# A two-layer hybrid decoder trunk on one core: the state-space products' small blocks as 256-column operands, and PSUM as four single and two double banks

## The chip, the cores and the metric

The kernel runs on one core of a Trainium2 chip. The metric is the time of one execution on the device, in microseconds (us); a smaller one is better.

## What is computed

A sequence of 512 tokens of width 2048 goes through two layers. Layer A is sparse attention: an indexer of 16 small heads scores all earlier tokens, each query keeps its best 128, and 16 heads attend over those. Layer B is a Mamba-2 mixer with 64 heads of width 64 and chunks of 128 tokens. The change touches the diagonal part of B's scan and a few accumulators of A. What B computes there is, from the reference:

```python
a_cs = jnp.cumsum(a_, axis=-1)
lmat = jnp.exp(segsum(a_))
cb = jnp.einsum('bclgn,bcsgn->bgcls', c_, b_)
y_diag = jnp.einsum('bgcls,bgrcls,bcsgrp->bclgrp', cb, lmat, x_)
...
return (y_diag + y_off).reshape(b, s, nh, p)
```

The kernel works with chunks of 256 tokens there (two blocks of 128), so a head has for each of two chunks an upper block (source tokens 0 to 127 of the chunk, 256 target tokens) and a small block (source tokens 128 to 255, 128 target tokens). The indexer of layer A, which the change touches as well, is

```python
dots = jnp.einsum('bqhd,bsd->bqsh', iqb, ik)
score = jnp.einsum('bqsh,bqh->bqs', jax.nn.relu(dots), iwb).astype(jnp.float32)
```

## The kernel before, in words

**Products.** Every float32 product is made of reduced-precision parts: an operand is split into a high part (a ScalarE copy) and a low part (a VectorE subtraction), and TensorE forms high·high, low·high and high·low. Most of the work are dense tiles of 128 output rows by 512 tokens, class `Dense`: 16 or 32 blocks of the inner dimension, three products each (L229 to L231), accumulated in one PSUM tile `acc`. Four such tiles at a time are made token by token for the values v (class `TokenMajor`, L265 to L267).

**Order.** The program is written out by hand: a main loop over units of four blocks, in which one tick is one block (`kk`). At each tick generator threads are stepped, which emit the evictions, the attention and the state-space work between the dense products. `yield n` puts off a thread by n ticks. Each engine runs its instructions in the order written, and the framework adds the semaphore waits. Weights are loaded by SyncE's queue into three `raw` buffers and split three units ahead (L206 on ScalarE, L90 on VectorE).

**PSUM.** Eight banks of 512 float32 columns in one pool, each tile one bank (`PS`, L77): `acc`, the indexer's `dots`, the attention's `sps`, `ptp`, `av`, the state-space tiles `xst`, `st`, `yo`, `cpa`, `cpb`, and `y0`, `y1`, `yc`. A new tile waits until the last reader of the bank's former tile is done.

**The places that matter here.**

- The first five dense tiles (indexer queries) are made together, unit by unit. As each ends, `evac_iq` (L382 to L390) copies and subtracts its upper and its lower 64 rows in turn: `iqa`, two ticks later `iqb`.
- `index_thread` (L406 on): for each of three query blocks and 16 heads one `dots` tile of two products (L424, L425), one tick later its relu on ScalarE (L428), two ticks later its share of the score on VectorE (L434).
- `TokenMajor.mm` (L259): the four token blocks b have an accumulator each. After the last unit's products of block b its eviction is emitted at once: `vh` on ScalarE (L498), two ticks later `vl` on VectorE (L500).
- `m_make` (L843) builds the mask tiles of head pair p, m = 0 and 1 for the upper blocks of both chunks, m = 2 for the two small blocks, splits each into `mh` and `ml`. `m_mul` (L874), when m = 2 is there, forms all products of the pair: eight into `y0` and `y1` (L886, L887), six into `yc` (L892 to L894), each of 256 columns. A pair's 128 rows of a stationary operand hold one head's high part in 64 and its low part in the other 64, so one product gives both. VectorE adds the pieces up (L906 and two adds a head).

Of the kernel before, what the change touches and what calls it, by code (L numbers as in the profile page):

```python
# [16 lines left out]
P = 128  # L17
# [25 lines left out]
def kernel(  # L43
# [23 lines left out]
    banks = ctx.enter_context(tc.tile_pool(name="banks", bufs=8, space=bass.MemoryType.PSUM))  # L67
# [9 lines left out]
    def PS(name):  # L77
        return banks.tile([P, S], F32, tag="s", name=name)

# [94 lines left out]
    class Dense:  # L174
        def __init__(self, src, ncol, nk, operand, evac, t0=0, t1=S, packed=False, early=None,
                     order=None, keep=(), given=None):
# [37 lines left out]
        def mm(self, u, kk):  # L214
            first = u == self.order[0] and kk == 0
            if first:
                self.acc = PS("acc")
            ts, m = slice(self.t0, self.t1), self.ncol
            out = self.acc[:, : self.t1 - self.t0]
            held = self.given.w if self.given and u in self.given.keep else self.w  # L220
            w = [a[:, kk] for a in held[u]]
            k = 4 * u + kk
            xh, xl = self.operand(k)
            last = u == self.order[-1] and kk == 3
            if self.packed:
                te.matmul(out[: 2 * m], w[2], xh[:, ts], start=first, stop=last, skip_group_check=True)
                te.matmul(out[:m], w[0], xl[:, ts], start=False, stop=last, skip_group_check=True)
            else:
                te.matmul(out[:m], w[0], xh[:, ts], start=first, stop=False)  # L229
                te.matmul(out[:m], w[0], xl[:, ts], start=False, stop=False)  # L230
                te.matmul(out[:m], w[1], xh[:, ts], start=False, stop=last)  # L231
            if kk == 3 and u not in self.keep:
                del held[u]
            if last:
                run(self.evac(out if self.packed else out[:m]))

    class TokenMajor:
# [168 lines left out]
    def index_thread(iw):  # L406
# [9 lines left out]
        for i in range(1, NB):  # L416
# [369 lines left out]
    def xdt_make(p, d2):  # L786
# [14 lines left out]
        highs, lows = (slice(0, 4, 3), slice(0, 2)), (slice(1, 3), slice(2, 4))  # L801
        for c in range(2):
            sc.copy(out=parts[c][:, :, highs[c]], in_=heads2(v)[:, c:4:2])
        yield HOP
        for c in range(2):
            sub(parts[c][:, :, lows[c]], heads2(v)[:, c:4:2], f(parts[c][:, :, highs[c]]))
# [36 lines left out]
    def m_make(p, m):  # L843
# [19 lines left out]
        hi, lo = T("mh", F32R), T("ml", F32R)  # L863
        yield 1
        yield from split(hi, lo, t)
# [8 lines left out]
    def m_mul(p, m, hi, lo):  # L874
        m_next[0] = (p, m + 1) if m < 2 else (p + 1, 0)
        m_tiles.setdefault(p, []).append((hi, lo))
        if m == 2:
            tiles_m = m_tiles.pop(p)
            ys, yc = [PS("y0"), PS("y1")], PS("yc")
            stat = lambda s, n: xdt[p][s % 2][:, 256 * (s // 2) + P * n : 256 * (s // 2) + P * (n + 1)]  # L880
            two = lambda a: a.rearrange("p (e l) -> p e l", e=2)
            for s, (hi, lo) in zip((0, 2), tiles_m):
                for e in range(2):
                    x = stat(s, e)
                    out = ys[e][:, 128 * s : 128 * s + 256]
                    te.matmul(out, x, hi[:, 256 * e : 256 * e + 256], start=s == 0, stop=False, skip_group_check=True)  # L886
                    te.matmul(out, x, lo[:, 256 * e : 256 * e + 256], start=False, stop=True, skip_group_check=True)  # L887
# [15 lines left out]
            odd = lambda a: a.rearrange("p (c h l) -> p c h l", h=2, l=P)  # L903
            for e in range(2):
                r, q = slice(64 * e, 64 * e + 64), slice(64 - 64 * e, 128 - 64 * e)
                ve.scalar_tensor_tensor(out=v[r], in0=x[r], scalar=col(C_D, p)[r], in1=ys[e][r],  # L906
                                        op0=ALU.mult, op1=ALU.add)
                yield 1
                add(v[r], v[r], ys[e][q])
                yield 1  # L910
                add(odd(v[r])[:, :, 1], odd(v[r])[:, :, 1], odd(yc[r])[:, :, e])
# [59 lines left out]
    def evac_ob(j):  # L971
        def go(ps):
            t = PS("x2p") if j >= KD - 5 else T("x2")
# [57 lines left out]
    EARLY_TILES = 5  # L1031
    for t in range(8):
        dense(wa[t], P, 16, opA, evac_iq(t), t0=P, early=t if t < EARLY_TILES else None)
# [219 lines left out]
```

## Time and profile before

| | |
|---|---|
| median of 3 executions | 2420.07 us (2419.6 to 2422.0) |
| the profiled execution | 2420.4 us, its span 2418.7 us |
| TensorE (PE) busy | 2403.6 us, 99% of the span |
| VectorE (DVE) busy | 1564.1 us, 65% |
| ScalarE (ACT) busy | 1060.4 us, 44% |
| granted TensorE clock, mean | 0.999 of full speed |

The profile comes from one execution. Matrix products overlap each other in it (a product of 512 columns is shown as 0.39 us long, but the next starts 0.23 us after it), so what a product costs is read from start to start. PEld is the loading of the stationary operand. "Idle before" is the time an engine stood still just before an instruction, with the instruction that ended it.

### The profile page before, as it was taken

To read this page: it belongs to the slowest core of one execution; us is meant where nothing else is said; L and a number is where in the kernel's file an instruction comes from. 1 tells how busy PE (TensorE), PEld (TensorE's weight loads), DVE (VectorE), ACT (ScalarE), POOL (GpSimd) and SP (SyncE) were. 2 spreads that over 40 slices of the span, in tenths; PEclk is the share of its full clock that TensorE was granted. 3 is DMA by queue.
4 is the path that set the end of the run, shared out by engine and by line. 5 is a ranking of instruction groups with operands and counts; after the bars stand their busy time and mean duration, and the time that the engine had idled before them with its cause. 6 is when DMAs were issued, how large, how long until landed. Compare 5 with 4: busy or idle time off the path is not lost.

```text
span 2418.7 us, 29767 instructions
## 1 busy us (share of the span) xinstructions
PE 2403.6 (99%) x11430; PEld 2019.1 (83%) x11430; DVE 1564.1 (65%) x2811; ACT 1060.4 (44%) x2102; POOL 1.2 (0%) x8
## 2 busy tenths in 40 slices
PE   9999999999999999999999999999999999999998
PEld 9888888888888888888888888888888888888887
DVE  6569455464554664448788888888888888433334
ACT  6433233232332443334556565565656566322222
POOL 0000000000000000000000000000000000000000
PEclk9999999999999999999999999999999999999999
DMA  6362222222222223433333333333334344332233
GB/s 223 101 131 88 107 93 80 85 91 89 93 81 84 90 105 135 152 118 126 128 104 125 118 122 123 127 128 102 125 111 140 114 148 157 127 113 100 101 113 109
DMA packets 83439, 278.53 MB, mean 115 GB/s; under 512 B 7745, under 2 KB 40929, under 8 KB 58209
## 3 DMA queue, kind: packets, MB, share of 16 engines
q1 hardware_dynamic: 78976, 266.41, 32.6%
q10 hardware_dynamic: 4320, 10.23, 1.2%
q8 instruction: 89, 1.46, 0.2%
q14 instruction: 54, 0.43, 0.1%
HBM read 258.32 MB, written 18.02 MB: 114 GB/s over the span
## 4 chain that ended last, share of the span: by engine, by line
PE 96%; DMA 2%; DVE 1%; ACT 0%; ACTq 0%; SPq 0%; issue 0%; DVEq 0%
PE acc L229 27%; PE acc L231 27%; PE acc L230 27%; PE acc L265 2%; PE acc L267 2%; PE acc L266 2%; DMA raw<-wa 2%; PE ptp L547 1%; PE y L887 1%; PE y L886 1%; PE xst L789 1%; DMA rawu<-wa 0%; PE av L563 0%; PE sps L518 0%; PE av L562 0%; PE sps L517 0%
## 5 line engine op out<-in xcount | busy, mean ns | idle before, releaser
L90 DVE TENSOR_TENSOR wl<-raw,wh 128x512 fp32r<-128x512 f32 (+1 forms) x788 | 528.5, 684 | 136.8 <-ACT wh L206 95.2
L206 ACT CAST wh<-raw 128x512 fp32r<-128x512 f32 (+1 forms) x724 | 426.3, 613 | 176.1 <-PE acc L230 100.9
L229 PE MATMUL acc<-x1h,wh 128*128 128x512 f32 x1280 | 503.1, 393 | 0.0
L230 PE MATMUL acc<-x1l,wh 128*128 128x512 f32 x1280 | 499.2, 390 | 0.0
L231 PE MATMUL acc<-x1h,wl 128*128 128x512 f32 x1280 | 498.9, 390 | 0.0
L229 PE MATMUL acc<-xh,wh 128*128 128x512 f32 (+2 forms) x912 | 353.0, 387 | 1.8 <-ACT wh L206 1.5
L231 PE MATMUL acc<-xh,wl 128*128 128x512 f32 (+2 forms) x912 | 349.4, 383 | 0.4 <-DVE wl L90 0.3
L230 PE MATMUL acc<-xl,wh 128*128 128x512 f32 (+2 forms) x912 | 349.2, 383 | 0.5 <-DVE xl L101 0.5
L231 PEld LDWEIGHTS acc<-x1h,wl 128*128 128x128 f32 x1280 | 240.3, 188 | 51.0
L229 PEld LDWEIGHTS acc<-x1h,wh 128*128 128x128 f32 x1280 | 240.7, 188 | 46.5
L230 PEld LDWEIGHTS acc<-x1l,wh 128*128 128x128 f32 x1280 | 240.8, 188 | 46.2
L229 PE MATMUL acc<-ygh,wh 128*128 128x512 f32 (+1 forms) x544 | 205.3, 377 | 0.0
L231 PE MATMUL acc<-ygh,wl 128*128 128x512 f32 (+1 forms) x544 | 204.9, 377 | 0.0
L230 PE MATMUL acc<-ygl,wh 128*128 128x512 f32 (+1 forms) x544 | 204.9, 377 | 0.0
L231 PEld LDWEIGHTS acc<-xh,wl 128*128 128x128 f32 (+1 forms) x912 | 170.6, 187 | 34.7 <-DVE wl L90 2.3
L229 PEld LDWEIGHTS acc<-xh,wh 128*128 128x128 f32 (+1 forms) x912 | 170.7, 187 | 32.0 <-ACT wh L206 2.1
L230 PEld LDWEIGHTS acc<-xl,wh 128*128 128x128 f32 (+1 forms) x912 | 170.9, 187 | 30.1 <-DVE xl L101 1.4
L231 PEld LDWEIGHTS acc<-ygh,wl 128*128 128x128 f32 x544 | 102.4, 188 | 18.8
L229 PEld LDWEIGHTS acc<-ygh,wh 128*128 128x128 f32 x544 | 102.4, 188 | 18.8
L230 PEld LDWEIGHTS acc<-ygl,wh 128*128 128x128 f32 x544 | 102.4, 188 | 18.5
L697 DVE SCALAR_TENSOR_TENSOR hh<-rw,cols,hh 128x511 f32<-128x511 f32 x144 | 107.4, 746 | 6.5 <-ACT hh L694 4.0
L857 ACT ACTIVATE bc<-bc,aloc 128x256 f32<-128x256 f32 (+1 forms) x256 | 102.8, 446 | 0.5
(279 smaller groups left out, 3297.3 us busy)
## 6 DMA issues: line engine op xcount, KB each, us to landing
raw<-wb SPq DMA_DIRECT2D x80, 1024.0 KB, 4.8
raw<-wa SPq DMA_DIRECT2D x48, 1024.0 KB, 4.9
raw<-wbo SPq DMA_DIRECT2D x33, 1024.0 KB, 4.8
bc<-r_scr SPq DMA_DIRECT2D x96, 256.0 KB, 6.1
raw<-wav SPq DMA_DIRECT2D x16, 1024.0 KB, 4.9
raw<-wao SPq DMA_DIRECT2D x16, 1024.0 KB, 5.2
yg_scr<-yy SPq DMA_DIRECT2D x24, 256.0 KB, 4.4
ygr<-yg_scr SPq DMA_DIRECT2D x24, 256.0 KB, 5.1
```

Source lines behind the costliest of these rows:

```text
L90: ve.tensor_tensor(out=out, in0=a, in1=b, op=ALU.subtract)
L206: sc.copy(out=self.w[u][0], in_=self.raw[u].rearrange("p (k j) -> p k j", k=4))
L229: te.matmul(out[:m], w[0], xh[:, ts], start=first, stop=False)
L230: te.matmul(out[:m], w[0], xl[:, ts], start=False, stop=False)
L231: te.matmul(out[:m], w[1], xh[:, ts], start=False, stop=last)
L265: te.matmul(out, xh[:, bs], wh, start=u == 0, stop=False)
L266: te.matmul(out, xh[:, bs], wl, start=False, stop=False)
L267: te.matmul(out, xl[:, bs], wh, start=False, stop=u == 15)
L547: te.transpose(ps[:, n + (i - j) * P : n + (i - j + 1) * P], prob[i][:, j * P : (j + 1) * P], ident)
L697: ve.scalar_tensor_tensor(out=hh[:, d:], in0=rw[:, : S - d], scalar=col(C_CW, 4 * ct + 3 - d), in1=hh[:, d:], op0=ALU.mult, op1=ALU.add)
L789: te.transpose(ps[:, c * P : (c + 1) * P], xs[p][:, c * P : (c + 1) * P], ident)
L857: sc.activation(out=t3[:, e, a:b], in_=t3[:, e, a:b], func=AF.Relu, scale=-1.0, bias=aloc[:, s, 2 * p + e : 2 * p + e + 1])
```

## The change

- `m_make` for m = 2 writes two tiles `m0` and `m1`, one a head, in which high and low part of each chunk's small block lie side by side: 256 columns for a chunk. That takes two ScalarE copies and two VectorE subtractions of 256 columns in place of one each of 512.
- `m_mul` forms four products with them in place of six. Each adds its high half to the second 128 columns of the upper block, and leaves its low half in 128 columns of its own. A head's results for a chunk take 384 columns of a bank, so `y` is two tiles of two banks.
- `xdt_make` writes the stationary parts in the same order for both chunks.
- PSUM becomes four single banks and two double ones (`PS2`). Besides `y`, the double ones hold: the first four dense tiles, two to a tile (`half_of_two`); the four accumulators of `TokenMajor`; the `dots` of two heads, whose four products are now emitted together; and four late tiles of the output projection's residual.

```diff
+    banks = ctx.enter_context(tc.tile_pool(name="banks", bufs=4, space=bass.MemoryType.PSUM))
...
+    def PS2(name):
+        return banks.tile([P, 2, S], F32, tag="y", name=name, bufs=2)
...
-                self.acc = PS("acc")
+                self.acc = self.bank() if self.bank else PS("acc")
...
-                self.acc = [PS("acc") for _ in range(NB)]
+                self.acc = [a[:, b] for a in (PS2("vacc"), PS2("vacc")) for b in range(2)]
...
-                q = iqhl[h // 2][h % 2]
-                qs = slice((i - 1) * P, i * P)
-                ps = PS("dots")
-                te.matmul(ps[:, :w], q[:, qs], hi[:, :w], start=True, stop=False)
-                te.matmul(ps[:, :w], q[:, qs], los[h % 2][:, :w], start=False, stop=True)
+                if h % 2 == 0:
+                    qs = slice((i - 1) * P, i * P)
+                    two = PS2("dots")
+                    for e in range(2):
+                        q = iqhl[h // 2][e]
+                        te.matmul(two[:, e, :w], q[:, qs], hi[:, :w], start=True, stop=False)
+                        te.matmul(two[:, e, :w], q[:, qs], los[e][:, :w], start=False, stop=True)
+                ps = two[:, h % 2]
...
+            hi, lo = T("m0", F32R), T("m1", F32R)
+            cut = lambda a: a.rearrange("p (c x l) -> p c x l", c=2, x=2)
+            src = t.rearrange("p (e c l) -> p e c l", e=2, c=2)
+            for e, a in enumerate((hi, lo)):
+                sc.copy(out=cut(a)[:, :, 0], in_=src[:, e])
+            yield HOP
+            for e, a in enumerate((hi, lo)):
+                sub(cut(a)[:, :, 1], src[:, e], f(cut(a)[:, :, 0]))
...
-            hi, lo = tiles_m[2]
-            for i, s in enumerate((1, 3)):
-                ls, out = slice(i * P, (i + 1) * P), two(yc[:, 256 * i : 256 * i + 256])
-                te.matmul(out, stat(s, 0), two(hi)[:, :, ls], start=i == 0, stop=False, skip_group_check=True)
-                te.matmul(out, stat(s, 0), two(lo)[:, :, ls], start=False, stop=False, skip_group_check=True)
-                te.matmul(out, stat(s, 1), two(hi)[:, :, ls], start=False, stop=i == 1, skip_group_check=True)
+            for c in range(2):
+                for e in range(2):
+                    te.matmul(ys[e][:, c, P : 3 * P], stat(2 * c + 1, e), tiles_m[2][e][:, 256 * c : 256 * c + 256],
+                              start=False, stop=True, skip_group_check=True)
...
+    both = []
+    def half_of_two():
+        if not both:
+            a = PS2("acc2")
+            both.extend([a[:, 0], a[:, 1]])
+        return both.pop(0)
```

**Place 1: TensorE, the last unit of the first four v accumulators.** Names are output<-operands, with buffer numbers; brackets name the semaphores that an instruction waits for, by the engine that counts them. Before, each block has a tile of its own:

```order
L265 MATMUL acc_2313<-wh_2538,xh_423 128x512 [waits Activation_49]
L266 MATMUL acc_2313<-wl_2539,xh_423 128x512 [waits DVE_49]
L267 MATMUL acc_2313<-wh_2538,xl_424 128x512
L265 MATMUL acc_2314<-wh_2538,xh_423 128x512
L266 MATMUL acc_2314<-wl_2539,xh_423 128x512
```

And now:

```order
L270 MATMUL vacc_2287<-wh_2510,xh_421 128x512 [waits Activation_49]
L271 MATMUL vacc_2287<-wl_2511,xh_421 128x512 [waits DVE_49]
L272 MATMUL vacc_2287<-wh_2510,xl_422 128x512
L270 MATMUL vacc_2287<-wh_2510,xh_421 128x512 [waits Activation_49]
L271 MATMUL vacc_2287<-wl_2511,xh_421 128x512
L272 MATMUL vacc_2287<-wh_2510,xl_422 128x512
L270 MATMUL vacc_2288<-wh_2510,xh_421 128x512
L271 MATMUL vacc_2288<-wl_2511,xh_421 128x512
L272 MATMUL vacc_2288<-wh_2510,xl_422 128x512
L270 MATMUL vacc_2288<-wh_2510,xh_421 128x512 [waits Activation_49]
```

The products stand in the same order. The first product of the second half of each double tile has a wait for ScalarE that it did not have.

**Place 2: TensorE, the last unit of the second indexer tile.** Before:

```order
L229 MATMUL acc_203<-xh_372,wh_489 128x384 [waits Activation_49]
L230 MATMUL acc_203<-xl_373,wh_489 128x384
L231 MATMUL acc_203<-xh_372,wl_490 128x384 [waits DVE_49]
L229 MATMUL acc_203<-xh_388,wh_489 128x384
L230 MATMUL acc_203<-xl_389,wh_489 128x384
```

And now, where tiles one and two are halves of `acc2_175`:

```order
L234 MATMUL acc2_175<-xh_370,wh_487 128x384 [waits Activation_49]
L235 MATMUL acc2_175<-xl_371,wh_487 128x384
L236 MATMUL acc2_175<-xh_370,wl_488 128x384 [waits DVE_49]
L234 MATMUL acc2_175<-xh_386,wh_487 128x384 [waits Activation_49]
L235 MATMUL acc2_175<-xl_387,wh_487 128x384
L236 MATMUL acc2_175<-xh_386,wl_488 128x384
L234 MATMUL acc2_175<-xh_405,wh_487 128x384
L235 MATMUL acc2_175<-xl_406,wh_487 128x384
L236 MATMUL acc2_175<-xh_405,wl_488 128x384
L234 MATMUL acc2_175<-xh_421,wh_487 128x384 [waits DVE_49]
```

The second and the fourth block of this unit have a wait now. The fourth tile, second half of `acc2_229`, has the same three.

**Place 3: TensorE, the indexer's `dots` of the second query block, heads 4 and 5.** Before, the even head's two products stand between dense ones, the odd head's two follow nine dense products later, and none of the four has a wait:

```order
L230 MATMUL acc_1409<-xl_373,wh_1405 128x512
L231 MATMUL acc_1409<-xh_372,wl_1406 128x512 [waits DVE_49]
L424 MATMUL dots_1509<-ikh_992,iqa_587 128x384
L425 MATMUL dots_1509<-ikla_993,iqa_587 128x384
L229 MATMUL acc_1409<-xh_388,wh_1405 128x512
L230 MATMUL acc_1409<-xl_389,wh_1405 128x512
```

And now:

```order
L235 MATMUL acc_1399<-xl_371,wh_1395 128x512
L236 MATMUL acc_1399<-xh_370,wl_1396 128x512 [waits DVE_49]
L431 MATMUL dots_1497<-ikh_990,iqa_585 128x384 [waits Activation_49]
L432 MATMUL dots_1497<-ikla_991,iqa_585 128x384
L431 MATMUL dots_1497<-ikh_990,iqb_586 128x384
L432 MATMUL dots_1497<-iklb_992,iqb_586 128x384
L234 MATMUL acc_1399<-xh_386,wh_1395 128x512
L235 MATMUL acc_1399<-xl_387,wh_1395 128x512
```

The odd head's two products moved up by nine dense products to the even head's, and the first of the four waits for ScalarE: the tile lies where `dots_1406`, heads 0 and 1, lay two tiles before.

## Rows read from the trace of the kernel before

**Rows 1.** The page: engines' busy time (share, instructions), and the chain's shares.

```profile
PE 2403.6 (99%) x11430; PEld 2019.1 (83%) x11430; DVE 1564.1 (65%) x2811; ACT 1060.4 (44%) x2102; POOL 1.2 (0%) x8
PE 96%; DMA 2%; DVE 1%; ACT 0%; ACTq 0%; SPq 0%; issue 0%; DVEq 0%
```

**Rows 2.** Busy time of a stretch: stretch, its length, PE, PEld, DVE, ACT.

```profile
1200.00:1900.00 700.00, 698.85 (x3405) 589.16 (x3403) 594.35 (x1003) 422.97 (x861) 0.00 (x0) 1.00 0.35 121
```

**Rows 3.** PE's waits: line, releaser, us in total, times, longest.

```profile
PE st L822 <- DVE xd2l L90: 1.1, 1, 1.1
```

**Rows 4.** Timeline of PE, one head pair's products: start, length, instruction.

```profile
1161.35 0.28 PE L886 MATMUL y<-mh,xdhl 128*128 128x256 f32 x1
...
1163.02 0.40 PE L229 MATMUL acc<-x1h,wh 128*128 128x512 f32 x1
```

**Rows 5.** Groups of instructions by line: xcount, busy us, mean ns, idle before.

```profile
L93 ACT CAST mh<-bc 128x512 fp32r<-128x512 f32 x96 | 59.6, 621 | 36.7 <-DVE bc L862 36.3
L803 ACT CAST xdhl<-xdt 128x256 fp32r<-128x256 f32 x64 | 22.7, 401 | 44.1 <-DVE xdt L793 44.1
L90 DVE TENSOR_TENSOR ml<-bc,mh 128x512 fp32r<-128x512 f32 x96 | 65.7, 685 | 6.9 <-ACT mh L93 5.5
L90 DVE TENSOR_TENSOR xdhl<-xdt,xdhl 128x256 fp32r<-128x256 f32 x64 | 24.1, 418 | 0.0
L892 PE MATMUL yc<-mh,xdhl 128*128 128x256 f32 x64 | 18.1, 283 | 0.0
```

**Rows 6.** Timeline of PE and ACT at the end of the first v tiles.

```profile
282.31 0.39 PE L267 MATMUL acc<-wh,xl 128*128 128x512 f32 x1
282.54 0.39 PE L265 MATMUL acc<-wh,xh 128*128 128x512 f32 x1
282.74 2.73 ACT L498 ACTIVATE vh<-acc,rcol 128x512 fp32r<-128x512 f32 x4 [24.92 <-PE acc L267]
```

**Rows 7.** Timeline of PE at the wait for late weights.

```profile
152.63 0.49 PE L229 MATMUL acc<-xh,wh 128*128 128x512 f32 x1 [1.03 <-ACT wh L206]
152.96 0.40 PE L230 MATMUL acc<-xl,wh 128*128 128x512 f32 x1
```

**Rows 8.** Timeline at the end of the first five tiles: starts of tiles two, three, five.

```profile
43.10 0.33 PE L229 MATMUL acc<-xh,wh 128*128 128x384 f32 x1
45.18 0.33 PE L229 MATMUL acc<-xh,wh 128*128 128x384 f32 x1
49.34 0.34 PE L229 MATMUL acc<-xh,wh 128*128 128x384 f32 x1
```

**Rows 9.** Timeline of ACT there: copies of tiles one, one, two, three, three.

```profile
43.30 0.47 ACT L386 CAST iqa<-acc 64x384 fp32r<-64x384 f32 x1 [6.42 <-PE acc L231]
...
44.39 0.47 ACT L386 CAST iqb<-acc 64x384 fp32r<-64x384 f32 x1
45.44 0.47 ACT L386 CAST iqa<-acc 64x384 fp32r<-64x384 f32 x1 [0.57 <-PE acc L231]
...
48.14 0.47 ACT L386 CAST iqa<-acc 64x384 fp32r<-64x384 f32 x1
...
49.46 0.47 ACT L386 CAST iqb<-acc 64x384 fp32r<-64x384 f32 x1 [0.32 <-DVE iqa L90]
```

**Rows 10.** Timeline of SyncE's queue, then ACT, then PE, around the late weights.

```profile
114.83 0.66 SPq L367 DMA_DIRECT2D bias_scr<-rs  x1
115.58 81.80 SPq L187 DMA_DIRECT2D raw<-wa  x7
...
151.96 0.62 ACT L206 CAST wh<-raw 128x512 fp32r<-128x512 f32 x1 [11.59 <-DMA raw<-wa]
152.48 0.48 ACT L428 ACTIVATE relu<-dots 128x384 f32<-128x384 f32 x1
...
148.68 0.33 PE L424 MATMUL dots<-ikh,iqa 128*128 128x384 f32 x1
```

**Rows 11.** Busy time of the stretch behind it, columns as in rows 2.

```profile
152.80:172.00 19.20, 19.10 (x83) 14.87 (x84) 18.72 (x52) 7.84 (x18) 0.00 (x0) 1.00 0.29 107
```

More of the change, by code (lines that the diff above doesn't have):

```diff
@@ L66 @@
     small = ctx.enter_context(tc.tile_pool(name="small", bufs=24))
-    banks = ctx.enter_context(tc.tile_pool(name="banks", bufs=8, space=bass.MemoryType.PSUM))
+    banks = ctx.enter_context(tc.tile_pool(name="banks", bufs=4, space=bass.MemoryType.PSUM))
     dram = ctx.enter_context(tc.tile_pool(name="dram", bufs=1, space=bass.MemoryType.DRAM))
@@ L175, in __init__ @@
         def __init__(self, src, ncol, nk, operand, evac, t0=0, t1=S, packed=False, early=None,
-                     order=None, keep=(), given=None):
+                     order=None, keep=(), given=None, bank=None):
+            self.bank = bank
             self.order = list(order or range(nk // 4))
@@ L800, in xdt_make @@
         parts = [a.rearrange("p (c x d) -> p c x d", x=4, d=64) for a in st]
-        highs, lows = (slice(0, 4, 3), slice(0, 2)), (slice(1, 3), slice(2, 4))
+        highs, lows = slice(0, 4, 3), slice(1, 3)
         for c in range(2):
-            sc.copy(out=parts[c][:, :, highs[c]], in_=heads2(v)[:, c:4:2])
+            sc.copy(out=parts[c][:, :, highs], in_=heads2(v)[:, c:4:2])
         yield HOP
         for c in range(2):
-            sub(parts[c][:, :, lows[c]], heads2(v)[:, c:4:2], f(parts[c][:, :, highs[c]]))
+            sub(parts[c][:, :, lows], heads2(v)[:, c:4:2], f(parts[c][:, :, highs]))
         xdt[p] = st
@@ L862, in m_make @@
         ve.tensor_tensor(out=t3, in0=t3, in1=cb[:, None, :].to_broadcast([P, 2, 256]), op=ALU.mult)
-        hi, lo = T("mh", F32R), T("ml", F32R)
         yield 1
-        yield from split(hi, lo, t)
+        if m < 2:
+            hi, lo = T("mh", F32R), T("ml", F32R)
+            yield from split(hi, lo, t)
+        else:
+            hi, lo = T("m0", F32R), T("m1", F32R)
[6 more added lines that the diff above has]
+                sub(cut(a)[:, :, 1], src[:, e], f(cut(a)[:, :, 0]))
         yield 8
@@ L878, in m_mul @@
             tiles_m = m_tiles.pop(p)
-            ys, yc = [PS("y0"), PS("y1")], PS("yc")
+            ys = [PS2("y") for _ in range(2)]
             stat = lambda s, n: xdt[p][s % 2][:, 256 * (s // 2) + P * n : 256 * (s // 2) + P * (n + 1)]
-            two = lambda a: a.rearrange("p (e l) -> p e l", e=2)
-            for s, (hi, lo) in zip((0, 2), tiles_m):
+            for c in range(2):
                 for e in range(2):
[L884 to L887, printed above, removed]
-            hi, lo = tiles_m[2]
-            for i, s in enumerate((1, 3)):
-                ls, out = slice(i * P, (i + 1) * P), two(yc[:, 256 * i : 256 * i + 256])
-                te.matmul(out, stat(s, 0), two(hi)[:, :, ls], start=i == 0, stop=False, skip_group_check=True)
-                te.matmul(out, stat(s, 0), two(lo)[:, :, ls], start=False, stop=False, skip_group_check=True)
-                te.matmul(out, stat(s, 1), two(hi)[:, :, ls], start=False, stop=i == 1, skip_group_check=True)
+                    y, es = ys[e][:, c], slice(256 * e, 256 * e + 256)
+                    for n, m_part in enumerate(tiles_m[c]):
+                        te.matmul(y[:, :256], stat(2 * c, e), m_part[:, es], start=n == 0, stop=False,
+                                  skip_group_check=True)
+            for c in range(2):
+                for e in range(2):
+                    te.matmul(ys[e][:, c, P : 3 * P], stat(2 * c + 1, e), tiles_m[2][e][:, 256 * c : 256 * c + 256],
+                              start=False, stop=True, skip_group_check=True)
             v = T("yy")
@@ L902, in m_mul @@
             yield 2
-            odd = lambda a: a.rearrange("p (c h l) -> p c h l", h=2, l=P)
+            cut = lambda a: a.rearrange("p (c l) -> p c l", c=2)
             for e in range(2):
                 r, q = slice(64 * e, 64 * e + 64), slice(64 - 64 * e, 128 - 64 * e)
-                ve.scalar_tensor_tensor(out=v[r], in0=x[r], scalar=col(C_D, p)[r], in1=ys[e][r],
+                ve.scalar_tensor_tensor(out=cut(v[r]), in0=cut(x[r]), scalar=col(C_D, p)[r], in1=ys[e][r, :, :256],
                                         op0=ALU.mult, op1=ALU.add)
                 yield 1
-                add(v[r], v[r], ys[e][q])
+                add(cut(v[r]), cut(v[r]), ys[e][q, :, :256])
                 yield 1
-                add(odd(v[r])[:, :, 1], odd(v[r])[:, :, 1], odd(yc[r])[:, :, e])
+                add(cut(v[r])[:, :, P:], cut(v[r])[:, :, P:], ys[e][r, :, 256 : 3 * P])
             add(v[:, late], v[:, late], t)
@@ L972, in go @@
         def go(ps):
-            t = PS("x2p") if j >= KD - 5 else T("x2")
+            t = half_of_two() if j >= KD - 5 else T("x2")
             residual_ob(t, ps, j, slice(0, S))
@@ L1031 @@
     EARLY_TILES = 5
+    both = []
[4 more added lines that the diff above has]
+        return both.pop(0)
     for t in range(8):
-        dense(wa[t], P, 16, opA, evac_iq(t), t0=P, early=t if t < EARLY_TILES else None)
+        dense(wa[t], P, 16, opA, evac_iq(t), t0=P, early=t if t < EARLY_TILES else None,
+              bank=half_of_two if t < 4 else None)
         if t == EARLY_TILES - 1:
```

## The prediction

> **What bounds the kernel now.** I read the page first: TensorE is busy 99% of the span, and 96% of the chain of waits is its own work [rows 1]. So a product removed is worth its whole spacing, and a wait added to TensorE its whole length, unless it was waiting there anyway. The stretch table comes next, for the state-space stage, where the new masks are made: TensorE is busy 698.85 of 700 us, VectorE 594.35, ScalarE 422.97 [rows 2]. The list of waits says that TensorE waits once in that stage, 1.1 us for VectorE [rows 3]. The other engines have room; the reader should look only for TensorE's products and its waits. Last I read timelines at the places where the order of the changed kernel has a wait of TensorE that the old one has not.
>
> **What is removed.** A head pair's 14 products run from 1161.35 to 1163.02, 0.119 us each [rows 4]. There are 12 now, for 32 pairs (a line of the `yc` group counts 64, two a pair [rows 5]): 64 × 0.119 = **7.6 us less**. The products left have the same 256 columns. Bounds 7.0 (64 × 0.11, should the shorter bursts keep more of their edges) and 7.7.
>
> **What is added off the path.** The third mask's split is two ScalarE copies and two subtractions of 256 columns instead of one of 512 each. A copy of 621 ns becomes 2 × 401, a subtraction of 685 ns 2 × 418 [rows 5]: 0.18 and 0.15 us a pair, 5.8 and 4.8 us in all. I cost this at nothing, since VectorE has some 105 us and ScalarE 277 us of room in 700 [rows 2]. If that cover were gone, VectorE's 4.8 us would be the price.
>
> **Three new waits on TensorE.** A wait costs a little over its length. After one, the next product started 0.33 us later (152.63 to 152.96 [rows 7]) where the regular step is 0.23 (282.31 to 282.54 [rows 6]): about 0.1 us of restart, since the next stationary operand isn't loaded ahead.
>
> *(a) The v accumulators (place 1).* Block b = 1 uses the operands that block 0 has just used, so its new wait for ScalarE can't be for an operand. What ScalarE does with that tile is `vh` of block 0: the framework treats the two banks as one tile. `vh` started at 282.74, when block 0's last product had ended, and four of them took 2.73 us, about 0.69 each [rows 6]. So block 1 starts at 282.74 + 0.69 + 0.05 = 283.48 instead of 282.54: 0.94, with the restart 1.05. Block 2 lies in the other tile and doesn't wait. Block 3 waits for block 2's `vh`, which comes after block 1's on ScalarE; the same sum gives 1.06. That is 2.1 us for each of four groups, **8.4 us**. ScalarE had stood idle for 24.92 us before the first [rows 6], so nothing is ahead of it. Bounds 7.5 (no restart) and 9.0. Behind the waiting product stand only further products; VectorE's `vl` comes later anyway.
>
> *(b) The first four dense tiles (place 2).* Tile two's first block now waits for `iqa` of tile one (43.30 + 0.47 = 43.77 [rows 9]) and starts at 43.82, not 43.10 [rows 8]. Its three products of 384 columns take 0.52 us (12 take 2.08, 43.10 to 45.18 [rows 8]) plus 0.1 restart, to 44.45; the second block waits for `iqb`, ended 44.86 [rows 9], and starts at 44.91. With 0.1 and nine more products the tile is done at 46.58 instead of 45.18: 1.4 us. The VectorE wait of the fourth block has passed by then. Tile three follows until 48.66. Its copy on ScalarE came 2.70 us after tile two's (45.44 to 48.14 [rows 9]), with squares and weight splits between, and tile two's now starts near 46.79; so it runs 49.49 to 49.96, and tile four starts at 50.01, 1.35 late. Its second block waits for `iqb`, which started 1.32 us behind `iqa` (48.14 to 49.46 [rows 9]) and so ends at 51.28. Nine products more, and tile five starts at 53.0 instead of 49.34 [rows 8]: **3.7 us**. Bounds 2.8 (the second pair costs what the first does) and 4.3 (the subtractions end last).
>
> *(c) The indexer (place 3).* With two double tiles, heads 4 and 5 need the tile of heads 0 and 1 back, that is head 1's relu. ScalarE runs in order, and stood 11.59 us before a weight copy whose load was late; head 1's relu came behind it, 152.48 to 152.96 [rows 10]. TensorE reaches the products at 148.68 [rows 10] and now stands until 153.01. Then 0.1 restart, four products of 0.174 and nine of 0.227 lead to 155.86, the point that it reached at 152.63 before [rows 7]: 3.2 us. That includes a gain, for the wait for those weights (1.03 [rows 7]) is gone. Some comes back: from 152.80 to 172 VectorE is busy 18.72 of 19.20 us, and TensorE's 83 products (69 of 0.227 and 14 of 0.174 are 18.1 us) waited about 1.1 us for it [rows 11]. A TensorE that is later finds its weights ready. So **2.1 us**, bounds 1.5 and 3.2.
>
> Do (b) and (c) add up? Late weights could swallow (b). The load is behind the `bias_scr` transfer in SyncE's queue (issued 114.83, the load 115.58 [rows 10]), which sends what TensorE's product of the bias table and VectorE made just before. It moves with TensorE, so they add.
>
> **Sum.** −7.6 + 8.4 + 3.7 + 2.1 = **+6.6 us**. The profiled execution took 2420.4 us (span 2418.7 and 1.7 around it), so 2427.0; it lies 0.3 above the median of the runs, 2420.07, so I forecast **2426.7 us** for a median. The bounds of the terms give +4.1 to +9.5, 2424.2 to 2429.6.
>
> **Rivals.**
>
> *The halves are free of each other (faster).* Here the new waits of (a) and (b) are for something long done. Place: the first product of the second half. It decides at 0.23 us: if that product starts one regular step behind the last of the first half, nothing is paid, and 2.1 − 7.6 gives 2414.6. For it: in the old trace `vh` reads one bank while products write the next, without a wait [rows 6]. Against it: the old order has no wait at that product, the new one has, and its operands are no reason. The Trainium skill ("PSUM — Partial Sum Buffer", section "Summary: rules for kernel authors") says that to read PSUM during products one should target a different bank, and guard by bank. By that rule block 1 owes block 0's eviction nothing, and the sum would be the rival's; rows 6 agree that the chip permits it. But a semaphore that the program waits for is waited for. Chance 0.05.
>
> *The late weights swallow the early delay (about the same).* If the load at 115.58 doesn't move with TensorE, (b) ends in the stop at 148.68 to 153.01, which stays where it is. Then −7.6 + 8.4 + 2.1 gives 2423.0. For it: seven loads stand in one piece from 115.58 on [rows 10]. Against it: the transfer ahead of them needs TensorE's result. Chance 0.08.
>
> *Four single banks are too few (slower still).* Dense accumulators, attention and state-space tiles now share four banks. Should one tile a head and a pair find its bank unread by 0.3 us, that is 48 × 0.4 us with restart, +19, 2446. For it: VectorE, which empties most banks, is 85% busy in the stage [rows 2]. Against it: `y` has left the common banks, and the one wait [rows 3] shows that VectorE is seldom behind. Chance 0.05.
>
> *The removed products save nothing (slower).* Should the pair's products end as late as before, because the first of `m0` waits for both copies and both subtractions, the waits stand alone: 2434.3. Against it: the products are emitted eight ticks behind the subtraction. Chance 0.04.
>
> **How the numbers follow.** The forecast keeps 0.78. About 0.2% (4.8 us) is what a measurement of this kernel can tell from no change, so slower begins at 2424.9, which nine tenths of the forecast's own spread lie above. Slower: 0.92 × 0.78 + 0.05 + 0.04 = 0.81; same: 0.06 + 0.08 = 0.14; faster 0.05. The range takes in the terms' bounds and the second rival, 2422.8 to 2429.4, and leaves the other three rivals out (0.14).
>
> **What would show it.** Right: four pairs of waits of about 1 us before `vacc` products, released by `vh`; waits for `iqa` and `iqb` near 44 and 50 us; one stop of some 4 us near 152 us for a relu; 128 `yc`-like products of 256 columns where there were 192; otherwise no new wait in the state-space stage. Wrong: products of block 1 one step behind block 0's; a stage from 1100 to 2000 us that isn't about 6 us shorter; waits of `acc`, `xst` or `sps` for a bank.

## The result: 0.64% slower, more than twice what was forecast

| | before | after |
|---|---|---|
| median, 6 executions each on one chip | 2420.54 us (2419.6 to 2422.0) | 2436.69 us (2433.89 to 2438.07) |
| ratio, 95% interval | | 1.0064 [1.0053, 1.0074] |
| the profiled execution, its span | 2420.4, 2418.7 us | 2435.83, 2434.1 us |

The forecast was 2426.7 us, with a range of 2422.8 to 2429.4. The sign is right, the time lies 7 us above the range. The page of the kernel after, busy time and the chain's shares, to be held against [rows 1]:

```profile
span 2434.1 us, 29648 instructions
PE 2402.8 (99%) x11366; PEld 2015.1 (83%) x11366; DVE 1566.8 (64%) x2843; ACT 1062.6 (44%) x2134; POOL 1.2 (0%) x8
PE 95%; DMA 2%; DVE 1%; ACT 1%; issue 0%; SPq 0%; ACTq 0%; DVEq 0%
```

TensorE has the 64 products less, and is busy about as long in a span that is 15.4 us longer. What it waits for stands in the list of its waits (line, releaser, us in total, times, longest); in the kernel before no single wait is longer than that of [rows 3]:

```profile
PE vacc L270 <- ACT vh L506: 6.4, 8, 0.8
PE dots L431 <- ACT relu L436: 5.0, 1, 5.0
PE acc L234 <- ACT iqb L391: 2.4, 2, 1.2
PE acc L234 <- ACT iqa L391: 1.7, 2, 1.2
PE acc L234 <- DVE iqb L94: 1.4, 2, 0.7
PE st L830 <- DVE xd2l L94: 1.1, 1, 1.1
```

All the new waits lie at the three places that the prediction named. To put a price on each place I matched the TensorE products that both kernels have and took how much later each starts in the profiled execution of after. That lateness is 0.1 us up to 43 us, 8.9 from 60 to 110, 14.3 from 241 to 296, 23.1 behind the last v tiles, and 15.4 at the end of the state-space stage.

| term | predicted | measured in the two traces |
|---|---|---|
| state-space stage, 64 products less | −7.6 | −7.6 |
| (a) v accumulators | +8.4 | +8.7 |
| (b) first four dense tiles | +3.7 | +8.8 |
| (c) the indexer's stop | +2.1 | +5.4 |
| sum | +6.6 | +15.3 |

**Place (a)**, timelines of PE and ACT in the kernel after (start, length, instruction, in brackets the idle time before it and what ended it). In [rows 6] the second block began 0.23 us after the first's last product; here:

```profile
296.64 0.39 PE L272 MATMUL vacc<-wh,xl 128*128 128x512 f32 x1
297.81 0.50 PE L270 MATMUL vacc<-wh,xh 128*128 128x512 f32 x1 [0.78 <-ACT vh L506]
...
297.07 0.69 ACT L506 ACTIVATE vh<-vacc,rcol 128x512 fp32r<-128x512 f32 x1 [24.82 <-PE vacc L272]
```

1.17 to 1.24 us from start to start in place of 0.23, eight times.

**Place (b)**, PE, then VectorE (DVE), then ScalarE, again of the kernel after; the tiles began regularly in [rows 8, 9]:

```profile
43.04 0.34 PE L236 MATMUL acc<-xh,wl 128*128 128x384 f32 x1
43.94 0.45 PE L234 MATMUL acc<-xh,wh 128*128 128x384 f32 x1 [0.56 <-ACT iqa L391]
...
45.96 0.45 PE L234 MATMUL acc<-xh,wh 128*128 128x384 f32 x1 [1.22 <-ACT iqb L391]
...
48.02 0.44 PE L234 MATMUL acc<-xh,wh 128*128 128x384 f32 x1 [0.72 <-DVE iqb L94]
...
56.13 0.69 PE L234 MATMUL acc<-xh,wh 128*128 128x384 f32 x1 [0.72 <-DVE iqb L94]
56.61 0.52 PE L235 MATMUL acc<-xl,wh 128*128 128x384 f32 x1
...
44.85 0.55 DVE L94 TENSOR_TENSOR iqa<-acc,iqa 64x384 fp32r<-64x384 f32 x1 [6.12 <-PE acc L236]
...
47.41 0.56 DVE L94 TENSOR_TENSOR iqb<-acc,iqb 64x384 fp32r<-64x384 f32 x1 [1.28 <-PE acc L236]
...
45.44 0.47 ACT L391 CAST iqb<-acc 64x384 fp32r<-64x384 f32 x1 [1.02 <-DVE iqa L94]
```

The bracket of the DVE row at 44.85 is the one to read. The subtraction of tile one's upper rows reads half 0, whose last product started at 43.04, yet it waits for TensorE's products at 43.94 to 44.40 into half 1. So the engines go in turns: the copy `iqa` lets the products of tile two's first block go (43.94, the end of the first stop), these let the subtraction go, that the copy `iqb` (45.44), and that the next products (45.96, the end of the second stop); these let the subtraction of `iqb` go (47.41), which ends the third stop (48.02). Each pair of tiles stops TensorE three times, in both pairs together 7.2 us.

The last PE rows show something else: the products from 56.13 on follow each other after 0.32 us, not 0.17. The stretch table of the kernel after (stretch, its length, PE, PEld, DVE, ACT, POOL, then the granted clock) says why:

```profile
43.00:56.00 13.00, 7.52 (x36) 5.59 (x34) 6.03 (x10) 6.19 (x12) 0.00 (x0) 1.00 0.00 0
56.00:59.30 3.30, 3.17 (x10) 3.17 (x11) 2.04 (x5) 1.78 (x4) 0.00 (x0) 0.50 0.00 0
161.80:168.60 6.80, 6.00 (x15) 5.04 (x16) 6.24 (x18) 3.53 (x8) 0.00 (x0) 0.50 0.36 152
168.60:280.00 111.40, 111.40 (x496) 92.71 (x496) 102.67 (x221) 40.63 (x78) 0.00 (x0) 1.00 0.30 103
```

TensorE, busy 7.52 of 13 us, then had half its clock (1.2 in place of 2.4 GHz) from 56 to 59.3 us. Before, the granted clock is 1.00 in the same stretches. That costs the other 1.6 us of (b): the lateness is 7.3 at 56.13 and 8.9 behind.

This second part differs from execution to execution. Five of the kernels below keep the six stops as they are, and their traces show the half clock there for 6.8 us (two kernels) or 13.7 us (three) in place of 3.4; (b) costs 9.2 to 12.2 us in them. The stretch table of one, the kernel with the bias table in pieces of 16 rows:

```profile
46.50:53.30 6.80, 6.08 (x19) 5.57 (x19) 2.93 (x5) 2.62 (x5) 0.00 (x0) 0.50 0.00 0
56.80:63.50 6.70, 5.98 (x19) 5.47 (x18) 3.65 (x6) 2.08 (x5) 0.00 (x0) 0.50 0.00 0
```

So 8.8 is the price in one execution, which is 0.9 us faster than the median of the six.

**Place (c)**, SyncE's queue, ScalarE and PE of the kernel after, to be held against [rows 10]:

```profile
123.91 0.66 SPq L372 DMA_DIRECT2D bias_scr<-rs  x1
...
161.53 0.62 ACT L211 CAST wh<-raw 128x512 fp32r<-128x512 f32 x1 [12.27 <-DMA raw<-wa]
162.06 0.48 ACT L436 ACTIVATE relu<-dots 128x384 f32<-128x384 f32 x1
...
157.23 0.39 PE L236 MATMUL acc<-xh,wl 128*128 128x512 f32 x1
162.60 0.69 PE L431 MATMUL dots<-ikh,iqa 128*128 128x384 f32 x1 [4.98 <-ACT relu L436]
163.08 0.52 PE L432 MATMUL dots<-ikla,iqa 128*128 128x384 f32 x1
```

The whole group moved: the bias transfer by 9.1 us, the copy that waits for the late load by 9.6. TensorE stops for 4.98 us, and then runs at the half clock (0.50 from 161.8 to 168.6, above).

### The profile page after: what moved, and what is told of

Same layout as the page of the kernel before. It is cut to its first block, busy times and chain, and to the rows that moved or that the text cites. A ratio compares the mean times of both kernels' runs of the same rounds, so it can differ in the third digit from the quotient of the medians.

```text
span 2434.1 us, 29648 instructions
## 1 busy us (share of the span) xinstructions
PE 2402.8 (99%) x11366; PEld 2015.1 (83%) x11366; DVE 1566.8 (64%) x2843; ACT 1062.6 (44%) x2134; POOL 1.2 (0%) x8
## 4 chain that ended last, share of the span: by engine, by line
PE 95%; DMA 2%; DVE 1%; ACT 1%; issue 0%; SPq 0%; ACTq 0%; DVEq 0%
PE acc L234 27%; PE acc L236 27%; PE acc L235 27%; PE vacc L270 2%; PE vacc L272 2%; PE vacc L271 2%; DMA raw<-wa 2%; PE y L906 1%; PE ptp L555 1%; DMA x<-xT 1%; PE y L910 1%; PE xst L797 1%; PE av L571 0%; PE sps L526 0%; PE av L570 0%; PE sps L525 0%
## 5 line engine op out<-in xcount | busy, mean ns | idle before, releaser
L270 PE MATMUL vacc<-wh,xh 128*128 128x512 f32 x256 | 102.6, 401 | 6.4 <-ACT vh L506 6.4
```

The lines of the kernel that those rows point to most:

```text
L270: te.matmul(out, xh[:, bs], wh, start=u == 0, stop=False)
```

## The experiments

Two theories were open on (b). **Two-way:** in a shared two-bank tile a reader of one half also waits for the products into the other half that were emitted ahead of it, so it is the order of emission that costs. **One-way** (my prediction's): only products wait, for readers. For (c), **L**: the stop comes from one late weight load behind the 3 MB bias transfer. For the clock, **K**: the fall follows the stops and costs time of its own; its rival is that the slow products lie beside other waits.

**No shared halves at the start.** The first two dense tiles take one half each of two double tiles, the next three single banks.

```diff
-              bank=half_of_two if t < 4 else None)
+              bank=(lambda: PS2("acc2")[:, 0]) if t < 2 else None)
```

> The changed kernel, but the first two dense tiles use one half each of two double tiles, tiles three to five single banks: no two accumulators share a tile. Theory T (two accumulators in one two-bank tile wait for each other's evictions, and between 43 and 60 us this and the clock that falls behind it cost the whole 9 us by which TensorE comes out later there): 8.5 to 9.5 us less than the changed kernel, 2427 to 2428, and TensorE reaches 100 us of the old program's time without delay. Rival S (my forecast's size was right for the shared tiles, 3.7 us, and the rest is due to something else at the start): about 4 us less, 2433.

**Shared halves, later evictions.** The tiles stay shared; the eviction of a first half is emitted five ticks later, behind the second half's last product.

```diff
-            if last:
+            if last and self.early in (0, 2):
+                spawn(self.evac(out[:m]), 5)
+            elif last:
                 run(self.evac(out if self.packed else out[:m]))
```

> The changed kernel, with the first four dense tiles in shared double tiles as it has them, but the first half's eviction emitted only after the second half's last product. Theory T (what costs is the order of emission: each wait stands between one half's read and the other half's product): TensorE's six waits between 43 and 57 us go, 8 to 9.5 us less, 2427 to 2429. Rival B (a read of one half beside a product into the other is slow in itself, bank by bank): 3 us less or nothing.

The first gave 2425.97 us (ratio to before 1.0021 [1.0011, 1.003]), the second 2425.58 (1.0021 [1.0012, 1.0031]): 10.7 and 11.1 us less than the changed kernel. Neither has a wait of TensorE left in 40 to 60 us. Both gains are past what was expected. In the traces the early loss falls from 8.8 us to 0.0 and 0.5, and the stop at the `dots` costs less as well: (c) is 3.9 and 4.4 us in place of 5.4. The stretch table of the second kernel at the start, to be held against the first stretch of after above:

```profile
43.00:56.00 13.00, 13.00 (x77) 13.00 (x76) 8.98 (x16) 9.09 (x19) 0.00 (x0) 1.00 0.00 0
```

TensorE is busy all the time, with the same banks shared. So sharing two banks costs nothing here; emitting a reader of one half ahead of the other half's products does.

**Evictions at once.** For the first four tiles all four instructions of an eviction are emitted together, with no products between.

```diff
-                yield HOP
+                if t >= 4:
+                    yield HOP
```

> The changed kernel, but for the first four dense tiles all four instructions of an eviction (copy of half a, subtraction from it, copy of half b, subtraction) are emitted together behind the tile's last product, instead of with pauses between them, in which products into the other half of the shared tile are emitted. Theory T (two-way: in a shared tile VectorE's subtraction also waits for TensorE's products into the other half that were emitted ahead of it, so the four instructions and the products go in turns): now nothing of an eviction waits for a product of the other half, but the other half's next product waits for the whole eviction, some 0.47 + 0.55 + 0.47 + 0.55 us less the product beside it, near 2 us, at each of the two pairs; of the 7.3 us of stops some 3 to 4 are left, the fall of the clock after them perhaps with it: 2 to 5 us less than the changed kernel, 2432 to 2435. Rival, the theory of my prediction (one-way: only TensorE's products wait, for the copies and subtractions ahead of them): a product then waits for four instructions in place of one or two, and this is dearer than the changed kernel, by 1 to 2 us, 2437.5 to 2439.

2434.45 us (ratio 1.0054 [1.004, 1.0067]), 2.2 us less than the changed kernel, where one-way asked for more; but the two intervals overlap, so it is the trace that decides. PE, then VectorE, then two rows of the stretch table, of this kernel:

```profile
45.37 0.44 PE L234 MATMUL acc<-xh,wh 128*128 128x384 f32 x1 [2.25 <-DVE iqb L94]
...
53.85 0.69 PE L234 MATMUL acc<-xh,wh 128*128 128x384 f32 x1 [2.46 <-DVE iqb L94]
...
43.67 0.55 DVE L94 TENSOR_TENSOR iqa<-acc,iqa 64x384 fp32r<-64x384 f32 x1 [5.21 <-ACT iqa L391]
...
46.90:50.30 3.40, 3.40 (x12) 3.40 (x11) 0.89 (x2) 1.30 (x3) 0.00 (x0) 0.50 0.00 0
53.70:57.10 3.40, 3.25 (x10) 3.25 (x11) 1.39 (x3) 0.68 (x2) 0.00 (x0) 0.50 0.00 0
```

One stop a pair in place of three, of 2.3 and 2.5 us, and the first subtraction now waits for its copy alone, 1.2 us earlier than at 44.85. That is two-way. By matched products the two stops cost 5.2 us in place of 7.2. Little of it reaches the time, because the half clock came behind both of them and costs 3.2 in place of 1.6.

**The v evictions last.** Those of all four blocks are emitted behind the last block's last product.

```diff
-            if u == 15:
-                run(self.evac(out, b))
+            if u == 15 and b == NB - 1:
+                for c in range(NB):
+                    run(self.evac(self.acc[c], c))
```

> The changed kernel, but the four v accumulators' evictions are emitted after the last block's last product, not each behind its own block. Theory T: the eight waits of 0.94 to 1.01 us with their restarts go, 8.4 us less, 2428, because no read of the shared tile stands ahead of a product in the program any more. Rival U (the evictions only move later, and the following q tile or the heads wait for v instead): less than 3 us less, with new waits of TensorE behind the v groups.

2427.71 us (1.0028 [1.0016, 1.004]), 9.0 less than the changed kernel. No wait of a `vacc` product is left, and none came in its place in 280 to 800 us.

**The bias table in pieces.** First in eight transfers of two heads:

```diff
-        sy.dma_start(out=dst, in_=rs[:HA, None, :384].to_broadcast([HA, P, 384]))
+        for c in range(0, HA, 2):
+            sy.dma_start(out=dst[c : c + 2], in_=rs[c : c + 2, None, :384].to_broadcast([2, P, 384]))
+            yield 16
```

> The changed kernel, but the bias table goes out in eight transfers of two heads, 16 ticks apart, instead of one of 16 heads. Theory L (the stop of 5.1 us at the indexer's products is head 1's relu behind a weight copy that waits for a load held up by the bias transfer; about 3 us more of it are TensorE's clock at half): the load comes in time, the stop and the half clock at 162 us go, 5 to 6.5 us less, 2430 to 2432. Rival W (two double tiles are too few for the indexer's dots whatever the load does): a stop of 3 us or more stays there.

This missed: 2439.11 us (1.0074 [1.0059, 1.0089]). The stop at the `dots` went, but others came further on. Waits of TensorE in this kernel, then the stretch table while a piece is written (the last two columns are the busy share of the 16 DMA engines and GB/s):

```profile
PE vacc L270 <- ACT wh L259: 4.5, 1, 4.5
...
PE acc L234 <- ACT wh L211: 2.2, 1, 2.2
```

```profile
139.00:145.00 6.00, 6.00 (x31) 5.04 (x31) 3.42 (x7) 1.78 (x5) 0.00 (x0) 1.00 0.12 35
```

A share of 0.12 is two engines of 16. The Trainium skill ("DMA: Bandwidth & Descriptors", section "Rules for kernel authors") says that an outermost dimension smaller than 16 confines a transfer to at most that many engines; the outermost here is the two heads, and the row agrees. So the pieces were cut the other way, 16 rows of the table for all 16 heads:

```diff
+        for c in range(0, P, 16):
+            sy.dma_start(out=dst[:, c : c + 16], in_=rs[:HA, None, :384].to_broadcast([HA, 16, 384]))
+            yield 16
```

> The changed kernel, but the bias table is written to memory in eight transfers of 16 of its 128 rows for all heads, with weights loaded between them; nothing else differs. Theory L (the stop of 5.0 us at the indexer's dots, with the fall of the granted clock behind it, comes from a raw weight load behind the one transfer of 3 MB): no stop there, granted clock 1.00 in 150 to 175, and 5.5 to 6.6 us less than the changed kernel (the two-part kernel lost 6.6 by the same edit), 2430 to 2431. Rival (the losses at the start delay TensorE by 9 us and had already covered part of the late load, so without the stop the wait turns up at a weight's copy further on): 2433 or above, the wait named in 200 to 260.

2428.31 us (1.0036 [1.0023, 1.0048]), 8.4 less than the changed kernel, and no stop at the `dots` (TensorE busy 25.00 of 25 us from 150 on). That is 2 us more than theory L allowed. A part is not (c)'s own, as the control shows, the kernel before with the same pieces:

> The kernel before, with the bias table written in the same eight transfers and nothing else changed: a control for the fastest kernel so far (2410.1), which holds the change and this edit. The trace of before shows stops of about 1.5 us in all in 148 to 153, given back in part; its clock does not fall there. Theory S: 0.5 to 2 us less than before, 2418.5 to 2420, so that the change without its sharing of halves is still worth 8 us or more. Rival (the edit, not the change, makes the fastest kernel fast): 2415 or below.

2418.03 us, ratio 0.9988 [0.9979, 0.9997]: 2.5 less than before, a little past what was expected, and far from the rival's 2415. By matched products the pieces bring TensorE forward by 2.5 us between 100 and 240 us both here and in the changed kernel, where (c) had set it back by 5.4. So nothing of (c) is left, and the 2.5 are the edit's own.

**A stop filled.** 20 idle products (float32 ones, which stand as 40 instructions in the trace) ahead of the `dots` at which the changed kernel stops:

```diff
+                    if i == 2 and h == 4:
+                        keep_warm(20)
```

> The changed kernel, with 20 idle 128-column products (their result is not used) emitted ahead of the two-bank tile of the third block's third pair of heads in the indexer, where TensorE stops for 5.0 us for the relu. They fill most of that stop with work on TensorE; the relu's wait for the late bias table and raw weights stays. Theory K (the fall of the granted clock to 0.5 from 161.8 to 168.6 costs some 3 us beside the stop itself, and it follows from TensorE's standing still): no fall of the clock there, granted clock 1.00 in 161 to 169, and some 2.5 to 3.3 us less than the changed kernel, 2433.4 to 2434.2. Rival (the stop itself is what costs; the slow products lie beside work that TensorE would have waited for): the time is that of the changed kernel within 0.7 us, 2436 to 2437.4, whether the clock falls or not.

2434.57 us (1.0052 [1.0039, 1.0064]), 2.1 less than the changed kernel, short of K's 2.5, and the two intervals overlap. TensorE's timeline in this kernel, and its stretch table:

```profile
157.69 4.63 PE L117 MATMUL warm<-ones 128*128 128x128 f32 x40
162.54 0.44 PE L433 MATMUL dots<-ikh,iqa 128*128 128x384 f32 x1 [0.23 <-ACT relu L438]
```

```profile
157.60:162.50 4.90, 4.72 (x42) 4.49 (x40) 0.37 (x1) 1.02 (x3) 0.00 (x0) 1.00 1.00 415
```

The `dots` start where they did (162.54 for 162.60), since the relu is as late. But the clock stays at 1.00, and matched products gain 3.0 us from there on (0.2 later than in the changed kernel from 60 us on, 2.8 earlier from 166 on), which is within K's range. That a fall costs time of its own rests on the trace, not on the medians.

**Products back.** 64 of the 256-column products run twice, into the same sums.

```diff
+                    for again in range(2 - e):
...
-                              start=False, stop=True, skip_group_check=True)
+                              start=False, stop=again == 1 - e, skip_group_check=True)
```

> The changed kernel, with 64 of its 256-column products done twice: of each pair of heads' four products with the small blocks' operand, the two of the first half of columns run a second time into the same sums (so the output differs). Term of the gain: 64 products at 0.119 us: 7.6 us more than the changed kernel, 2443.5 to 2445, all of it in the state-space stage. Rival (products in that stage lie partly beside waits, and the stage is shorter for its smaller number of VectorE and ScalarE instructions): under 5 us more.

2444.81 us (1.0099 [1.0085, 1.0113]): 8.1 more than the changed kernel, as the gain's term said; by matched products the state-space stage is 7.7 longer. The group of these products by line, in the kernel after and in this one:

```profile
L910 PE MATMUL y<-m,xdhl 128*128 128x256 f32 x128 | 20.6, 283 | 0.0
```

```profile
L911 PE MATMUL y<-m,xdhl 128*128 128x256 f32 x192 | 28.3, 283 | 0.0
```

**Two parts out.** No shared halves at the start, and v evictions last, by the two edits above.

> The changed kernel with two parts taken out: the first two dense tiles have a double tile each of which they use one half, the next three single banks, so no half is shared there; and the four accumulators of a v group are evicted only after the last block's last product. The state-space products and the indexer's dots are as in the changed kernel. Theory S (the three losses are separate and add up): the changed kernel's 2436.7 less 10.7 and less 9.0 as each did alone, 2417.0, of which the gain of the state-space stage (7.5) stands against the stop at the indexer's dots (5.5): faster than the kernel before by 1 to 4 us. Rival (the losses stand in for one another: without the early ones TensorE arrives sooner at a weight or a relu and waits there): 2420 or above, with the wait named in the chain in 140 to 260.

2416.71 us (0.9982 [0.9973, 0.9991]): the losses add, to 0.3 us. This kernel has one stop of TensorE longer than 1.1 us, 5.67 us at the `dots`. The same kernel with 24 idle products (48 instructions):

> The kernel with two parts taken out (no sharing of halves at the start, v evictions last; 2416.7), which has one stop, 5.7 us at the indexer's dots, and one fall of the granted clock, to 0.5 from 146.8 to 153.6 and past it; with 24 idle 128-column products (their result is not used) emitted ahead of the two-bank tile at which it stops. Theory K: the products fill the stop, the granted clock stays at 1.00, the relu's wait stays, and the time is 2 to 3.3 us less, 2413.4 to 2414.7. Rival (the slow products cost nothing, since TensorE would have waited behind them): 2416 to 2417.4.

2415.74 us (0.9979 [0.9971, 0.9988]): 1.0 less, half of what K asked for at least. The edit doesn't quite do what was written: it sets the idle products at h == 2, one pair of heads ahead of the stop, which is at heads 4 and 5 here too. TensorE so comes to that stop later, and waits 0.20 us there. TensorE in the two-part kernel, then in the one with the filler:

```profile
154.36 0.69 PE L432 MATMUL dots<-ikh,iqa 128*128 128x384 f32 x1 [5.67 <-ACT relu L437]
...
142.51 5.52 PE L117 MATMUL warm<-ones 128*128 128x128 f32 x48
...
153.05 0.44 PE L434 MATMUL dots<-ikh,iqa 128*128 128x384 f32 x1 [0.20 <-ACT relu L439]
```

The stretch with the stop, of the two-part kernel, then of the one with the filler:

```profile
150.00:158.00 8.00, 3.64 (x10) 3.20 (x11) 3.98 (x11) 3.80 (x8) 0.00 (x0) 0.57 0.66 277
```

```profile
150.00:158.00 8.00, 7.80 (x36) 6.24 (x35) 5.23 (x14) 3.69 (x8) 0.00 (x0) 1.00 0.51 215
```

The granted clock fell without the filler and not with it, so that half of K stands. The price was read off the wrong stretch: in the two-part kernel the clock is at 0.50 from 151.0 to 157.8 us, not from 146.8 to 153.6, so about half of the fall lies under the stop itself, and only nine products behind it were slow. Matched products gain 1.7 us there, less than K's 2; why the medians differ by 1.0 only, one trace of each doesn't show.

**All three out.** The two parts, and the bias table in pieces of 16 rows.

> The same two parts taken out, and the bias table written to memory in eight transfers of 16 of its 128 rows each, for all 16 heads, instead of one transfer of 3 MB, so that weights are loaded between them. Theory S with L (the stop at the indexer's dots comes from ScalarE's copy of weights, queued ahead of the relu and waiting for a raw load behind the 3 MB transfer): no stop there, no fall of the clock, 5 to 6 us less than with the two parts alone, 2411 to 2413, faster than both kernels. Rival (the pieces run slowly, as those of two heads each did, and hold up loads behind them): the stop moves to a weight's copy in 200 to 260, and the time is 2416 or above.

2410.11 us (2409.07 to 2410.88), ratio 0.9954 [0.9941, 0.9966]: faster than both kernels. Its page and its stretch at the former stop:

```profile
PE 2394.1 (99%) x11366; PEld 2011.0 (83%) x11366; DVE 1566.5 (65%) x2843; ACT 1062.2 (44%) x2134; POOL 1.2 (0%) x8
...
PE 98%; DMA 1%; DVE 1%; SPq 0%; ACT 0%; issue 0%; ACTq 0%; DVEq 0%
```

```profile
147.00:175.00 28.00, 28.00 (x130) 23.72 (x129) 24.92 (x63) 10.69 (x23) 0.00 (x0) 1.00 0.35 104
```

Transfers issued in 90 to 160 us (number, size, median us to landing), in the kernel after:

```profile
raw<-wa SPq DMA_DIRECT2D x5, 1024.0 KB, 17.0
bias_scr<-rs SPq DMA_DIRECT2D x1, 3072.0 KB, 33.6
```

And in this one:

```profile
raw<-wa SPq DMA_DIRECT2D x6, 1024.0 KB, 5.4
bias_scr<-rs SPq DMA_DIRECT2D x5, 384.0 KB, 6.3
```

Against the kernel before with the same pieces (2418.03) it is 7.9 us faster: that is what the change is worth without its waits, and the 7.6 of the 64 products.

## Why the prediction was right and wrong

- **What is removed: right.** 7.6 predicted, 7.6 between the traces, 8.1 with the products put back, 7.9 in the fastest kernel. The added copies and subtractions cost nothing, as said.
- **(a): right,** in place, releaser, number and price: 8.7 by matched products, 9.0 when taken out. The rival that the halves are free of each other is refuted by 0.78 us a wait. The Trainium skill ("PSUM — Partial Sum Buffer", section "Summary: rules for kernel authors") asks for a guard by bank; the waits here go by the tile of two banks, and the measurement decides.
- **(b): wrong, and the largest miss.** The step that failed is "The VectorE wait of the fourth block has passed by then". It took `iqb`'s subtraction to run as in the kernel before. But VectorE waits too: the sum had TensorE's new waits and none of VectorE's. In place of two stops a pair there are three, 7.2 us in all instead of 3.7. This could have been read blind. The prediction showed the order of TensorE alone; in the order of VectorE the first subtraction has a wait for TensorE that it lacked before:

```
L90 TENSOR_TENSOR iqa_539<-acc_175,iqa_539 64x384 [waits Activation_49]
```

```
L94 TENSOR_TENSOR iqa_537<-acc2_175,iqa_537 64x384 [waits PE_49,Activation_49]
```

- **(c): right in mechanism, mis-sized.** One stop, for a relu, behind the late weight load. Matched products are 7.5 us later right behind it (9.1 to 16.6, both read where the odd head's two products have moved ahead), of which 5.1 are the stop (157.23 to 162.60, less the regular 0.23) and some 2.4 the half clock, and 1.9 come back further on, 1.0 of it the wait for the weights that stood there before. The prediction had 4.2, and gave 2.1 back. In other kernels' traces that keep the stop, (c) costs 3.9 to 5.0.
- **The clock, in no term.** 1.6 us of (b) and 2.4 of (c) are TensorE at half its clock after it had stopped. That is 4.0 of the 8.7 us by which the sum was short in these two traces; 3.5 more are (b)'s third stop and the turns, 0.9 the longer stop of (c), 0.3 the waits of (a).
- **(b) and (c) add up: right.** The bias transfer moved by 9.1 us, as TensorE did, so the rival that late weights swallow the delay is out. So are the other two: no tile waits for a single bank in the list of waits, and the stage is shorter by what the products cost.
- **The range was too narrow at the top** because each bound varied one wait's length. None allowed for another wait or for slower products behind one. (The range's top also lies 0.2 below the 2429.6 that the terms' own bounds give.)

## What to carry to other kernels

Where two tiles become one, look at every engine's order, not only at the bound engine's: each reader of one half that stands ahead of products into the other half can make a wait in both directions. Emitted behind the last write to the whole tile, such readers made no wait here, and the sharing itself cost nothing. On an engine that is busy 99%, price a stop of some us at its length and at the slower products behind it, and look for filler or another order ahead of it.

## What the runs showed of the hardware

The granted clock of TensorE, 1.00 throughout the body of the kernel before, fell to 0.50 behind the chains of short stops at the start, behind two single stops of 2.3 and 2.5 us there (evictions at once), and beside every single stop of 4.5 to 5.7 us that wasn't filled; a stop of 2.2 us at 240 us, in the kernel with the table in pieces of two heads, brought no fall. The eight waits of about 0.8 us at the v accumulators brought none. Where the long stop was filled with idle products the clock stayed at 1.00 there, and the fastest kernel has no fall.

What a fall costs is only what TensorE does at the lower level: 1.7 us where half of the 6.8 us of the fall lay under the stop, 3.0 where products ran in 6.0 of 6.8 us. The same six stops at the start were followed by 3.4 us at the half clock in one trace and by 6.8 or 13.7 us in others.

A transfer of 3 MB from 16 partitions took 33.6 us, and the 1 MB weight loads around it landed after 17.0 us at the median. With the transfer in eight parts over the same 16 partitions and weights between them, the loads landed after 5.4 us, and TensorE had no wait from 40 to 800 us.
